# Where ScalarE writes an exp whose values nobody reads: SBUF rows in place of the PSUM bank it reads

## Chip, cores, metric

One core of a Trainium2 chip. The metric is device time in microseconds (us) of one execution; medians with lowest and highest are given.

## The reference

```python
def reference(x, bias):                       # x: (8, 2048, 2048) f32, bias: (8, 256)
    x_heads = x.reshape(B, S, H, Dh).transpose(0, 2, 1, 3)
    x_heads = x_heads + bias[None, :, None, :]
    x_tiled = np.repeat(x_heads, 2, axis=2)
    mx = x_tiled.max(axis=-1, keepdims=True)
    return mx.squeeze(-1) + np.log(np.exp(x_tiled - mx).sum(axis=-1))
```

A log of a sum of exps over each 256 elements of x + bias, every result given twice. The kernels take the exp without subtracting the maximum.

## The kernel before

It streams x, 134.2 MB, through nine SBUF buffers of 2 MiB: 64 blocks of 128 partitions x 2 rows x 2048 columns (8 heads of 256). The work on a block is split over the engines. In the first 49 blocks:

- Heads 0 and 1 ("ScalarE's own"): TensorE adds the bias by a bf16 matmul of ones with three bias parts, then an fp32 matmul of x with the identity into the same PSUM bank; ScalarE takes the exp, and the sum comes out of its accumulator.
- Heads 2 and 3: one large exp on ScalarE in place, VectorE multiplies by exp(bias) and sums.
- Heads 4 to 7: GpSimd adds the bias, the same large exp, VectorE sums.

Blocks 49 to 60 give ScalarE one head of its own, the last three blocks two.

```python
NBUF = 9
...
xts = [sb.tile([P, K, D], F32, name=f"xt{i}") for i in range(NBUF)]
ps = [pp.tile([P, MM], F32, name=f"ps{i}") for i in range(5)]     # five banks, in turn
...
def load(t):
    after = last_uses[t - NBUF] if t >= NBUF else []
    ...                                            # the load of block t waits for these
def add_bias(m, t, k0, k1):
    ...                                            # bias matmul, then x matmul, into bank p
        last_uses[t].append(on_x(t, mm, [loads[t, k0, 0]]))
    return got

def sum_biased(m, p, dst):
    for h in range(m["pe"]):
        c = h * Dh
        nc.scalar.activation(
            out=p[:, c : c + Dh],                  # in place in PSUM; never read
            in_=p[:, c : c + Dh],
            func=ACT.Exp,
            accum_out=dst(h),
        )
```

The softmax here doesn't subtract the row's maximum and nothing guards it: scores larger than these inputs give would overflow.

Of the kernel before, what the change touches and what calls it, by code (L numbers as in the profile page):

```python
# [16 lines left out]
NBUF = 9  # L17
# [15 lines left out]
def kernel(  # L33
# [6 lines left out]
    nc = tc.nc  # L40
    P = nc.NUM_PARTITIONS
    B, S, D = x.shape
    H, Dh = bias.shape
# [27 lines left out]
    xts = [sb.tile([P, K, D], F32, name=f"xt{i}") for i in range(NBUF)]  # L71
# [5 lines left out]
    def mode_of(t):  # L77
        return [m for t0, m, _ in STAGES if t0 <= t][-1]
# [4 lines left out]
    def pieces(t):  # L83

        if not halves_of(t):
            return [(0, K, 0, D)]
        cuts = [[0, D]] * K if t < T - 1 else LAST_CUTS
        return [
            (k, k + 1, c0, c1) for k in range(K) for c0, c1 in zip(cuts[k], cuts[k][1:])
        ]  # L90
# [13 lines left out]
    def on_x(t, ins, after):  # L104
        known = [u for u in users[t] if u.ins.engine != ins.ins.engine]
        for before in range(t % NBUF, t, NBUF):
            known += users[before]
        for u in known:
            if u not in after:
                tc.declare_no_dep(  # L110
                    ins.ins, u.ins, reason="waited for by those it waits for"
                )
        users[t].append(ins)
        return ins

    loads = {}

    last_uses = [[] for _ in range(T)]

    def load(t):  # L120
        after = last_uses[t - NBUF] if t >= NBUF else []
        for k0, k1, c0, c1 in pieces(t):
            loads[t, k0, c0] = on_x(
                t,
                nc.sync.dma_start(
                    out=xts[t % NBUF][:, k0:k1, c0:c1],
                    in_=rows_of(t)[:, k0:k1, c0:c1],
                ),
                after,
            )  # L130
# [37 lines left out]
    for i, c in enumerate(range(G0, D, MM)):  # L168
        spread(ps[i], c, c + MM)
        nc.scalar.activation(  # L170
            out=b_rep[:, c - G0 : c - G0 + MM], in_=ps[i], func=ACT.Copy
# [9 lines left out]

    def add_bias(m, t, k0, k1):

        n = m["pe"] * Dh
        xt = xts[t % NBUF]
        step = MM // n
        groups = [(k, min(k + step, k1)) for k in range(k0, k1, step)]
        got = []
        for ka, kb in groups:
            p = ps[n_ps[0] % len(ps)]  # L190
            n_ps[0] += 1
            nc.tensor.matmul(  # L192
                p[:, 0 : (kb - ka) * n],
                lhsT=ones3,
                rhs=each_row(b3, 0, n, kb - ka),
                start=True,
                stop=False,
            )
            got += [p[:, k * n : (k + 1) * n] for k in range(kb - ka)]
        for ka, kb in groups:  # L200
            p = got[ka - k0]
            mm = nc.tensor.matmul(  # L202
                bass.AP(
                    tensor=p.tensor,
                    offset=p.offset,
                    ap=[p.ap[0], [1, (kb - ka) * n]],
                ),
                lhsT=ident,
                rhs=xt[:, ka:kb, 0:n],
                start=False,  # L210
                stop=True,
            )
            last_uses[t].append(on_x(t, mm, [loads[t, k0, 0]]))
        return got

    def sum_biased(m, p, dst):
        for h in range(m["pe"]):
            c = h * Dh
            nc.scalar.activation(  # L219
                out=p[:, c : c + Dh],  # L220
                in_=p[:, c : c + Dh],
                func=ACT.Exp,
                accum_out=dst(h),
            )

    def each_row(src, c, n, k_rows):

        return bass.AP(
            tensor=src.tensor,
            offset=src.offset + c,  # L230
            ap=[src.ap[0], [0, k_rows], [1, n]],
        )

    def g_add(m, t, k0, k1):
        c = m["g0"] * Dh
        v = xts[t % NBUF][:, k0:k1, c:D]
        add = nc.gpsimd.tensor_tensor(  # L237
            out=v, in0=v, in1=each_row(b_rep, c - G0, D - c, k1 - k0), op=ALU.add
        )
        return on_x(t, add, [loads[t, k0, 0]])  # L240

    def exp_inplace(t, v, after):
        return on_x(t, nc.scalar.activation(out=v, in_=v, func=ACT.Exp), [after])  # L243

    def later(m, t, k0, k1, sums, add):

        h0 = m["pe"] if m["late"] else m["g0"]
        v = xts[t % NBUF][:, k0:k1, h0 * Dh : D]
        done = exp_inplace(t, v, add)
        if m["late"]:  # L250
            n = (m["g0"] - h0) * Dh
            f = v[:, :, 0:n]
            mul = nc.vector.tensor_tensor(  # L253
                out=f,
                in0=f,
                in1=each_row(w_ps, h0 * Dh - W0, n, k1 - k0),
                op=ALU.mult,
            )
            done = on_x(t, mul, [done])
        red = nc.vector.tensor_reduce(  # L260
            out=sums[:, k0:k1, h0:H],
            in_=v.rearrange("p k (h j) -> p k h j", j=Dh),
            op=ALU.add,
            axis=mybir.AxisListType.X,
        )
        last_uses[t].append(on_x(t, red, [done]))

    def weigh(t, v, h, dst, after):
        c = h * Dh
        w = w_ps[:, c - W0 : c - W0 + Dh] if c < W1 else w_sb[:, c - W1 : c - W1 + Dh]  # L270
        ttr = nc.vector.tensor_tensor_reduce(  # L271
            out=v,
            in0=v,
            in1=w,
            scale=1.0,
            scalar=0.0,
            op0=ALU.mult,
            op1=ALU.add,
            accum_out=dst,
        )  # L280
        last_uses[t].append(on_x(t, ttr, [after]))

    def finish(b):

        nr = H * NBLK
        tp = tps[b % 2]
        for k in range(K):
            nc.tensor.transpose(  # L288
                out=tp[0:nr, k],
                in_=R[b][:, k].rearrange("p h n -> p (h n)"),  # L290
                identity=ident,
            )
        tv = bass.AP(
            tensor=tp.tensor,
            offset=tp.offset,
            ap=[[tp.ap[0][0], nr], [1, P], [P, K], [0, 2]],
        )
        nc.scalar.activation(out=res[:, b], in_=tv, func=ACT.Ln)  # L298
# [23 lines left out]
    def sums_of(t):  # L322

        b, blk = divmod(t, NBLK)
        if b < B - 1:
            return R[b][:, :, :, blk]
        return R_last[:, :, blk, :].rearrange("p h k -> p k h")
# [3 lines left out]
    for t in range(T):  # L331
        m = mode_of(t)
        xt = xts[t % NBUF]
        sums = sums_of(t)
        for k0, k1, c0, c1 in pieces(t):
            add = None
            if c0 == 0:
                got = add_bias(m, t, k0, k1)
                if m["g0"] < H:
                    add = g_add(m, t, k0, k1)  # L340
            if for_pool:
                for_pool()
                for_pool = None
            h0 = max(c0 // Dh, m["pe"])
            h1 = min(c1 // Dh, m["g0"])
            if h0 < h1 and not m["late"]:
                done = exp_inplace(
                    t, xt[:, k0:k1, h0 * Dh : h1 * Dh], loads[t, k0, c0]
                )
            if for_pe and (c0 == 0 or c1 == D):  # L350
                for_pe()
                for_pe = None
            if not m["late"]:
                for k in range(k0, k1):
                    for h in range(h0, h1):
                        weigh(
                            t,
                            xt[:, k, h * Dh : (h + 1) * Dh],
                            h,
                            sums[:, k, h : h + 1],  # L360
                            done,
                        )

            def pool_part(t=t, m=m, k0=k0, k1=k1, sums=sums, add=add):
                if add:
                    later(m, t, k0, k1, sums, add)
                if k1 == K and t + NBUF < T:
                    load(t + NBUF)

            def pe_part(m=m, got=got, k0=k0, k1=k1, sums=sums):  # L370
                for k in range(k0, k1):
                    sum_biased(m, got[k - k0], lambda h: sums[:, k, h : h + 1])

            for_pool = pool_part
            if c0 == 0:
                if m["g0"] < H:
                    pe_part()
                else:
                    for_pe = pe_part

        fb, at = divmod(t - 2, NBLK)
        if fb >= 0 and at == NBLK - 1:
            finish(fb)
            if fb == B - 2:
                store()
# [34 lines left out]
```

## Time and profile before

| | kernel before |
|---|---|
| time, median (lowest to highest) | 329.37 us (329.17 to 329.44), 6 runs |
| span of the profiled run | 327.8 us |
| queue of the loads | 97.7% of the 16 DMA engines' time |
| ScalarE (ACT) busy | 290.7 us (89%) |
| VectorE (DVE), GpSimd (POOL), TensorE (PE) busy | 288.2, 270.7, 224.6 us |

Busy times of engines lie beside each other; none of them is the time. The lines behind the table stand in the prediction, with how they are read.

### The profile page before, as it was taken

How to read it: one execution, taken by the hardware profiler on the slowest of the kernel's cores; microseconds unless marked ns; L12 is line 12 of the kernel's file. 1: busy time of each engine (PE TensorE's matmuls, PEld its weight loads, DVE VectorE, ACT ScalarE, POOL GpSimd, SP SyncE). 2: the span in 40 equal slices, each digit the busy share in tenths (PEclk: the TensorE clock that was granted, in tenths of full speed). 3: DMA queues.
4: the chain of work that ended last, by engine and by line, in shares of the span. 5: the costliest groups of instructions: out<-in, count | busy, mean ns of one | idle time of the engine just before them, and what ended most of it. 6: DMA issues, size and time to landing. Idle time of an engine off the chain costs nothing.

```text
span 327.8 us, 1984 instructions
## 1 busy us (share of the span) xinstructions
PE 224.6 (68%) x383; PEld 65.2 (20%) x383; DVE 288.2 (88%) x380; ACT 290.7 (89%) x567; POOL 270.7 (83%) x79
## 2 busy tenths in 40 slices
PE   5497856667687668947897767687657546576793
PEld 2032211122122212211221211122212101122220
DVE  0009999999999999989999999999998999999994
ACT  3269999999999998999989899999998998999894
POOL 6999989979999999999998999999989668687300
PEclk9999798598967895698558777967897555555555
DMA  7999999999999999999999999999999999999991
GB/s 291 438 426 436 419 430 432 426 432 420 432 430 425 436 420 431 426 430 433 420 434 421 431 430 420 436 426 428 434 419 436 426 428 419 421 420 425 415 386 40
DMA packets 11646, 135.41 MB, mean 413 GB/s; under 512 B 1329, under 2 KB 1457, under 8 KB 2673
## 3 DMA queue, kind: packets, MB, share of 16 engines
q1 hardware_dynamic: 11536, 135.27, 97.7%
q8 instruction: 3, 0.05, 0.1%
q14 instruction: 9, 0.07, 0.1%
q10 hardware_dynamic: 2, 0.01, 0.0%
q0 software_dynamic: 96, 0.00, 0.0%
HBM read 134.23 MB, written 1.05 MB: 413 GB/s over the span
## 4 chain that ended last, share of the span: by engine, by line
DMA 66%; DVE 21%; ACT 4%; PE 4%; POOL 3%; issue 0%; SPq 0%; DVEq 0%
DMA xt<-in_x_dram 64%; DVE R L260 15%; DVE xt L253 5%; PE ps L202 3%; ACT xt L243 3%; DMA b<-bparts 2%; POOL xt L237 1%; ACT ps L219 1%; DMA brow<-in_bias_dram 1%; DVE xt L271 1%; PE ps L192 1%; POOL brest L157 0%; POOL brest L155 0%; POOL b L160 0%; POOL bparts L156 0%
## 5 line engine op out<-in xcount | busy, mean ns | idle before, releaser
L237 POOL TENSOR_TENSOR xt<-xt,b_rep 128x2048 f32<-128x2048 f32 (+2 forms) x65 | 264.3, 4069 | 33.2 <-DMA xt<-in_x_dram 33.2
L202 PE MATMUL ps<-xt,ident 128*128 128x512 f32 (+1 forms) x240 | 172.1, 848 | 77.4 <-DMA xt<-in_x_dram 77.1
L243 ACT ACTIVATE xt<-xt 128x3072 f32<-128x3072 f32 (+3 forms) x89 | 184.7, 2095 | 9.1 <-POOL xt L237 7.2
L260 DVE TENSOR_REDUCE R<-xt 128x12 f32<-128x3072 f32 (+1 forms) x56 | 176.6, 3154 | 1.7
L219 ACT ACTIVATE ps<-ps 128x256 f32<-128x256 f32 x232 | 85.7, 369 | 15.4 <-PE ps L202 11.4
L253 DVE TENSOR_TENSOR xt<-xt,w_ps 128x1024 f32<-128x1024 f32 x49 | 59.6, 1217 | 32.6 <-ACT xt L243 32.5
L202 PEld LDWEIGHTS ps<-xt,ident 128*128 128x128 f32 x240 | 53.3, 251 | 157.0 <-DMA xt<-in_x_dram 116.0
L192 PE MATMUL ps<-b,ones 3*128 3x512 bf16 (+1 forms) x120 | 47.1, 456 | 10.6 <-ACT ps L219 6.6
L219 ACT ACTIVATION_READ_ACCUMULATOR ps<-ps 128x1 f32 x232 | 44.1, 190 | 0.0
L271 DVE CUSTOM_DVE_ANT_0 xt<-xt,w_ps 128x256 f32<-128x256 f32 x114 | 40.4, 413 | 0.7 <-ACT xt L243 0.7
L192 PEld LDWEIGHTS <-ones 3*128 3x128 bf16 x120 | 7.8, 97 | 78.6 <-issue 78.6
L260 DVE TENSOR_REDUCE R_last<-xt 128x3 f32<-128x768 f32 (+1 forms) x9 | 9.3, 1036 | 0.0
L288 PE MATMUL tpair<-ident,R 128*64 128x128 f32 x14 | 3.7, 361 | 6.2 <-DVE R L260 6.2
L271 DVE CUSTOM_DVE_ANT_0 xt<-xt,w_sb 128x256 f32<-128x256 f32 x18 | 6.6, 416 | 0.0
L164 PE MATMUL ps<-brow,ones 1*128 1x512 f32 x4 | 3.7, 1085 | 3.4 <-DMA brow<-in_bias_dram 3.4
L271 DVE DVE_READ_ACCUMULATOR2_ANT R_last<- 128x1 f32 x76 | 6.0, 79 | 0.0
L170 ACT ACTIVATE b_rep<-ps 128x512 f32<-128x512 f32 x2 | 1.2, 598 | 4.5 <-PE ps L164 4.5
L271 DVE DVE_READ_ACCUMULATOR2_ANT R<- 128x1 f32 x56 | 4.6, 82 | 0.0
L164 PE MATMUL w_ps<-brow,ones 1*128 1x512 f32 x4 | 4.0, 1094 | 0.7 <-ACT w_ps L176 0.7
L288 PEld LDWEIGHTS tpair<-ident,R 128*64 128x64 f32 x14 | 1.6, 140 | 12.6 <-DVE R L260 10.0
L176 ACT ACTIVATE w_ps<-w_ps 128x512 f32<-128x512 f32 x2 | 1.2, 582 | 3.3 <-PE w_ps L164 3.3
L298 ACT ACTIVATE res<-tpair 64x512 f32<-64x512 f32 x7 | 4.0, 577 | 0.0
(21 smaller groups left out, 12.4 us busy)
## 6 DMA issues: line engine op xcount, KB each, us to landing
xt<-in_x_dram SPq DMA_DIRECT2D x57, 2048.0 KB, 31.9
xt<-in_x_dram SPq DMA_DIRECT2D x12, 1024.0 KB, 24.7
out_dram<-res SPq DMA_DIRECT2D x1, 896.0 KB, 9.8
xt<-in_x_dram SPq DMA_DIRECT2D x3, 256.0 KB, 14.4
xt<-in_x_dram SPq DMA_DIRECT2D x2, 384.0 KB, 16.1
xt<-in_x_dram SPq DMA_DIRECT2D x1, 512.0 KB, 12.2
out_dram<-res_last SPq DMA_DIRECT2D x1, 128.0 KB, 1.7
b<-bparts POOLq DMA_DIRECT2D x3, 1.0 KB, 5.9
```

The source lines that it names most:

```text
L164: nc.tensor.matmul(dst, lhsT=ones, rhs=brow[:, c0:c1], start=True, stop=True)
L170: nc.scalar.activation(out=b_rep[:, c - G0 : c - G0 + MM], in_=ps[i], func=ACT.Copy)
L192: nc.tensor.matmul(p[:, 0 : (kb - ka) * n], lhsT=ones3, rhs=each_row(b3, 0, n, kb - ka), start=True, stop=False,)
L202: mm = nc.tensor.matmul(bass.AP(tensor=p.tensor, offset=p.offset, ap=[p.ap[0], [1, (kb - ka) * n]],), lhsT=ident, rhs=xt[:, ka:kb, 0:n], s ...
L219: nc.scalar.activation(out=p[:, c : c + Dh], in_=p[:, c : c + Dh], func=ACT.Exp, accum_out=dst(h),)
L237: add = nc.gpsimd.tensor_tensor(out=v, in0=v, in1=each_row(b_rep, c - G0, D - c, k1 - k0), op=ALU.add)
L243: return on_x(t, nc.scalar.activation(out=v, in_=v, func=ACT.Exp), [after])
L253: mul = nc.vector.tensor_tensor(out=f, in0=f, in1=each_row(w_ps, h0 * Dh - W0, n, k1 - k0), op=ALU.mult,)
L260: red = nc.vector.tensor_reduce(out=sums[:, k0:k1, h0:H], in_=v.rearrange("p k (h j) -> p k h j", j=Dh), op=ALU.add, axis=mybir.AxisListTy ...
L271: ttr = nc.vector.tensor_tensor_reduce(out=v, in0=v, in1=w, scale=1.0, scalar=0.0, op0=ALU.mult, op1=ALU.add, accum_out=dst,)
L288: nc.tensor.transpose(out=tp[0:nr, k], in_=R[b][:, k].rearrange("p h n -> p (h n)"), identity=ident,)
L298: nc.scalar.activation(out=res[:, b], in_=tv, func=ACT.Ln)
```

## The change

The exp of ScalarE's own heads is an output that nobody reads; only its sum is wanted. The change sends it to the columns of x it came from, in SBUF, rather than back into the PSUM bank. The intent is to make the bank something that ScalarE only reads. In exchange ScalarE becomes a user of the x buffer, so the next load into it waits for ScalarE in place of the matmul. The core of the diff:

```diff
@@ add_bias @@
-            got += [p[:, k * n : (k + 1) * n] for k in range(kb - ka)]
+            got.append([p[:, k * n : (k + 1) * n] for k in range(kb - ka)])
 ...
-            last_uses[t].append(on_x(t, mm, [loads[t, k0, 0]]))
-        return got
-
-    def sum_biased(m, p, dst):
+            on_x(t, mm, [loads[t, k0, 0]])
+            rows += [(v, mm) for v in views]
+        return rows
+
+    def sum_biased(m, t, k, p, mm, sums):
+
         for h in range(m["pe"]):
             c = h * Dh
-            nc.scalar.activation(
-                out=p[:, c : c + Dh],
+            act = nc.scalar.activation(
+                out=xts[t % NBUF][:, k, c : c + Dh],
                 in_=p[:, c : c + Dh],
                 func=ACT.Exp,
-                accum_out=dst(h),
-            )
+                accum_out=sums[:, k, h : h + 1],
+            )
+            last_uses[t].append(on_x(t, act, [mm]))
```

More of the change, by code (lines that the diff above doesn't have):

```diff
@@ L198, in add_bias @@
             )
-            got += [p[:, k * n : (k + 1) * n] for k in range(kb - ka)]
-        for ka, kb in groups:
-            p = got[ka - k0]
+            got.append([p[:, k * n : (k + 1) * n] for k in range(kb - ka)])
+        rows = []
+        for (ka, kb), views in zip(groups, got):
+            p = views[0]
             mm = nc.tensor.matmul(
@@ L368, in pool_part, with pe_part @@
                     load(t + NBUF)
-            def pe_part(m=m, got=got, k0=k0, k1=k1, sums=sums):
+            def pe_part(t=t, m=m, got=got, k0=k0, k1=k1, sums=sums):
                 for k in range(k0, k1):
-                    sum_biased(m, got[k - k0], lambda h: sums[:, k, h : h + 1])
+                    sum_biased(m, t, k, *got[k - k0], sums)
             for_pool = pool_part
```

## The prediction

> **What bounds the kernel now.** I read the page from the top: busy shares, traffic by slice, queue shares.
>
> ```profile
> PE 224.6 (68%) x383; PEld 65.2 (20%) x383; DVE 288.2 (88%) x380; ACT 290.7 (89%) x567; POOL 270.7 (83%) x79
> GB/s 291 438 426 436 419 430 432 426 432 420 432 430 425 436 420 431 426 430 433 420 434 421 431 430 420 436 426 428 434 419 436 426 428 419 421 420 425 415 386 40
> q1 hardware_dynamic: 11536, 135.27, 97.7%
> ```
>
> ScalarE has the largest busy share of the compute engines, which makes the change look like one to the bottleneck. The two lines below it say otherwise: from the second slice of 8.2 us to the last but one the traffic stays between 386 and 438 GB/s, and the queue of the loads takes 97.7% of the time of the 16 DMA engines. No engine reaches that. Next the busy time by stage, to see whether the rate of the transfers depends on what the engines do (columns: stretch, then us in it, busy us and instructions of PE, PEld, DVE, ACT, POOL, granted clock, DMA share, GB/s).
>
> ```profile
> 8.00:16.00 8.00, 3.34 (x5) 0.63 (x4) 0.00 (x0) 1.91 (x3) 7.98 (x5) 1.00 1.00 426
> 16.00:25.00 9.00, 9.00 (x18) 2.76 (x16) 1.04 (x1) 5.59 (x14) 8.40 (x3) 1.00 1.01 433
> 25.00:87.00 62.00, 41.58 (x83) 12.14 (x82) 61.51 (x28) 60.99 (x124) 56.60 (x13) 0.86 1.01 428
> 87.00:165.00 78.00, 57.10 (x98) 16.67 (x98) 73.97 (x34) 73.17 (x150) 72.34 (x17) 0.75 1.01 428
> 165.00:295.00 130.00, 85.67 (x145) 24.52 (x144) 123.07 (x183) 119.73 (x219) 111.15 (x29) 0.70 1.01 426
> ```
>
> With ScalarE 24% busy (1.91 of 8.00 us) the rate is 426 GB/s; with ScalarE 98% busy (60.99 of 62.00) it is 428. Neither the load on ScalarE nor its SBUF traffic shows in it. 134.2 MB at 428 GB/s is 314 us, which is nearly the 315.2 us at which the last load on the chain lands. So the time is loads, and about 12.6 us of tail behind them.
>
> Then whether loads can ever be late, from the waits of the DMA queue's own issuer and the table of issues (KB each, us to landing):
>
> ```profile
> SPq L125 <- DVE R L260: 233.6, 50, 19.2
> xt<-in_x_dram SPq DMA_DIRECT2D x57, 2048.0 KB, 31.9
> ```
>
> A load is issued when the reduction on VectorE frees its buffer (233.6 us of waiting), but then takes 31.9 us to land, and at 428 GB/s a block of 2 MiB takes 4.90 us. So 31.9 / 4.90 = 6.5 blocks are in flight of nine buffers. A release would have to come some 27 us late before the DMA engines ran dry.
>
> **What the change touches.** Line 219 on ScalarE, 232 heads. In the steady part (time order: start, us, what):
>
> ```profile
> 154.07 0.37 ACT L219 ACTIVATE ps<-ps 128x256 f32<-128x256 f32 x1
> ...
> 154.58 0.37 ACT L219 ACTIVATE ps<-ps 128x256 f32<-128x256 f32 x1
> ...
> 154.96 0.38 ACT L219 ACTIVATE ps<-ps 128x256 f32<-128x256 f32 x1
> ...
> 155.47 0.37 ACT L219 ACTIVATE ps<-ps 128x256 f32<-128x256 f32 x1
> ```
>
> The starts are 0.51, 0.38 and 0.51 us apart. The lists of instructions of the two built programs tell why they alternate: in the kernel before, the second head of each bank waits for ScalarE's own semaphore, because its in-place output lies in the bank that the first head wrote. In the changed kernel that wait is gone: 114 ScalarE instructions waited for their own engine before (112 of them second heads), none after. The orders on TensorE, VectorE and GpSimd are the same; on the issuing queue the order is the same, and the loads wait for ScalarE where they waited for TensorE.
>
> **What the Trainium skill says.** "ScalarE: Activation LUTs", section "Step-by-step: what each stage is for", says that ScalarE writes faster to PSUM than to SBUF; by it the change goes the wrong way. "Perfetto Trace Analysis", section "Optimizing Scalar/DVE Operations", puts the access overhead of ScalarE at about 93 ns on SBUF and 51 ns on PSUM, 42 ns apart. The trace agrees with the direction but shows less (busy us, mean ns):
>
> ```profile
> L219 ACT ACTIVATE ps<-ps 128x256 f32<-128x256 f32 x232 | 85.7, 369 | 15.4 <-PE ps L202 11.4
> L170 ACT ACTIVATE b_rep<-ps 128x512 f32<-128x512 f32 x2 | 1.2, 598 | 4.5 <-PE ps L164 4.5
> L176 ACT ACTIVATE w_ps<-w_ps 128x512 f32<-128x512 f32 x2 | 1.2, 582 | 3.3 <-PE w_ps L164 3.3
> L315 ACT ACTIVATE res_last<-tpair 128x256 f32<-128x256 f32 x1 | 0.4, 384 | 1.2 <-PE tpair L309 1.2
> ```
>
> For 512 elements out of PSUM, a write to SBUF takes 598 ns and one to PSUM 582; for 256 elements 384 and 369. The destination alone costs 15 to 16 ns. "SBUF — State Buffer", section "Who interferes with whom", says that DMA has ports of its own and never contends with a compute engine; the stages above agree (426 to 433 GB/s). "DMA: Bandwidth & Descriptors", section "Where 436 GB/s comes from", gives a ceiling of 435 GB/s for the ports into SBUF; the trace's 428 is 98% of it, so nothing is left to win there.
>
> **The change part by part.**
> - Removed: 112 waits of ScalarE for itself, 0.51 - 0.38 = 0.13 us each: 14.6 us of ScalarE's time.
> - Added: 232 writes to SBUF in place of PSUM at 15 ns: 3.5 us, if all of it lies between starts. As the read of the accumulator already starts 0.28 to 0.30 us after its ACTIVATE and so overlaps the 0.37, I expect most of it not to.
> - Busy time: about 0.03 us of each 0.13 was an uncounted gap (the read of 0.18 to 0.19 us after 154.37 ends before 154.58), so 112 x 0.10 = 11 us of busy time go and up to 3.5 come back. ACT should show about 280 us in place of 290.7.
> - Moved: what frees a buffer. A block's heads end about 156 us in the stretch above, its large exp starts at 156.31 and its reduction ends at 163.7, so ScalarE's new claim is over some 7 us before the old one that counts. No load is issued later for it.
> - On the path: between the first block and 315 us, nothing. In the stage from 25 to 87 us, where the kernel catches up on its late start, the chain runs through VectorE without a gap (61.51 of 62.00 us busy), and VectorE's work is not changed; afterwards each block waits for its load.
>
> The tail is where ScalarE stands on the chain: from 315.25 us, where a large exp starts on landed data, to 321.88, where the last row of VectorE work starts.
>
> ```profile
> 317.81 2.08 PE L202 MATMUL ps<-xt,ident 128*128 128x512 f32 x2
> 318.43 1.56 ACT L243 ACTIVATE xt<-xt 128x768 f32<-128x768 f32 x2
> ...
> 319.92 0.37 ACT L219 ACTIVATE ps<-ps 128x256 f32<-128x256 f32 x1
> ...
> 320.81 1.56 ACT L243 ACTIVATE xt<-xt 128x1024 f32<-128x1024 f32 x2
> ...
> 321.88 0.42 DVE L271 CUSTOM_DVE_ANT_0 xt<-xt,w_ps 128x256 f32<-128x256 f32 x1 [0.44 <-ACT xt L243]
> ```
>
> Ahead of 321.88 lie three pairs of heads (starting at 316.64, 317.54 and 319.92), so three waits of 0.13 us, 0.39 us at most. But TensorE, at clock 0.50, ends the matmuls for the third pair at 317.81 + 2.08 = 319.89. ScalarE starts that pair at 319.92 today and would be ready for it 0.26 us earlier; it will wait there for TensorE instead. Only the third pair's own wait is left: 0.13 us. The last pair (322.46) is off the chain already. VectorE has 0.44 us to spare before 321.88, so it passes the 0.13 on.
>
> Sum: 329.38 - 0.13 = 329.25 us; I say **329.2**.
>
> **Rivals.**
> 1. ScalarE is the bound and its 11 us come off the time: about 318 us. For it: 89%, the largest share. Against it: the loads' 97.7%, and 314 us of transfers that no ScalarE time shortens. I give it under 1%.
> 2. The write to SBUF costs the skill's 42 ns between starts and nothing is won from the waits. ScalarE's work for a block is then 2.66 us (large exp, 61.60 to 64.26 us elsewhere in the trace) plus 2 x (0.51 + 0.38) + 4 x 0.042 = 4.61 us, under the 4.90 us of a block's load: hidden still, though above VectorE's 4.51 us a block (25.22 to 29.73) while catching up. In the tail six heads would add 0.25 us: 329.6.
> 3. ScalarE's 30 MB of new writes (232 x 128 KiB) into the rows that DMA fills slow the loads. One per cent of rate would be 3.1 us: 332.5. The stages speak against it, since the large exps write far more to SBUF (L243: 184.7 us of work) at an unchanged 428.
> 4. The third pair in the tail isn't held by TensorE (a higher clock at that stage): the full 0.39 us comes off, 329.0.
>
> **Range and chances.** Rivals 2 and 4 span 329.0 to 329.6. The three runs of before span 0.27 us, and executions otherwise differ by about 0.3%, which is 1 us and outweighs every step above. So 328.3 to 330.2. A 2% change is 6.6 us, which no step can make: faster 0.01, slower 0.01.
>
> **What would show it.** Right: load queue still near 97.7%, stages at 426 to 433 GB/s, starts of heads 0.38 us apart throughout, the heads' ACTIVATE at about 384 ns, ACT busy near 280 us with its idle time grown by as much and ended by GpSimd, TensorE or loads; and in the tail a pair of heads waiting for TensorE. Wrong: a lower GB/s in stages where heads run, heads still 0.51 us apart, loads whose issuer waits for ScalarE, or a span outside 325 to 331 us.

## The result and the profile after

329.25 us (328.67 to 329.45, 6 runs) after 329.37 (329.17 to 329.44, 6 runs). The ratio is 0.9994, 95% interval 0.9981 to 1.0007: the same. Here and below a ratio is the mean time of one kernel's runs over that of the other's of the same rounds, so it isn't quite the ratio of the medians quoted.

First the page of the changed kernel: busy times, traffic by slice, queue of the loads.

```profile
PE 227.0 (69%) x383; PEld 66.3 (20%) x383; DVE 288.4 (88%) x380; ACT 278.1 (85%) x567; POOL 270.8 (83%) x79
GB/s 293 431 428 434 427 426 428 428 424 432 426 426 431 426 430 425 426 432 425 424 433 424 423 432 426 430 430 424 428 429 422 434 428 416 422 418 423 420 394 52
q1 hardware_dynamic: 11536, 135.27, 97.8%
```

ScalarE lost 12.6 us of busy time (290.7 to 278.1). TensorE shows 2.4 us more (224.6 to 227.0), VectorE and GpSimd are within 0.2 us, and the load queue stays where it was (97.7%, now 97.8%). By stage (columns as in the prediction):

```profile
25.00:87.00 62.00, 42.34 (x80) 12.45 (x79) 61.55 (x28) 58.05 (x127) 56.99 (x13) 0.84 1.01 428
87.00:165.00 78.00, 57.62 (x100) 16.74 (x100) 73.43 (x33) 68.90 (x146) 72.27 (x17) 0.76 1.01 428
165.00:295.00 130.00, 87.69 (x143) 25.09 (x142) 122.86 (x182) 114.34 (x217) 111.02 (x29) 0.67 1.01 426
```

ScalarE is 3, 4 and 5 us less busy in the three stages; the rates, 428, 428 and 426 GB/s, are those of before. Then four heads of one block in order of time (start, us, what), to be held against the four in the prediction:

```profile
158.75 0.36 ACT L223 ACTIVATE xt<-ps 128x256 f32<-128x256 f32 x1
...
159.11 0.37 ACT L223 ACTIVATE xt<-ps 128x256 f32<-128x256 f32 x1
...
159.46 0.38 ACT L223 ACTIVATE xt<-ps 128x256 f32<-128x256 f32 x1
...
159.82 0.39 ACT L223 ACTIVATE xt<-ps 128x256 f32<-128x256 f32 x1
```

The steps are 0.36, 0.35 and 0.36 us where they were 0.51, 0.38 and 0.51. Counted over the whole trace, where no other engine was waited for between a head and the next, 113 of 150 steps were 0.50 to 0.53 us before, among them all 112 within a bank; now 139 of 144 are 0.35 to 0.38. The mean step within a bank fell from 0.516 to 0.361 us.

Last the tail, third pair of heads and what follows:

```profile
317.64 1.94 PE L204 MATMUL ps<-xt,ident 128*128 128x512 f32 x2
317.94 1.57 ACT L248 ACTIVATE xt<-xt 128x768 f32<-128x768 f32 x2
...
319.62 0.38 ACT L223 ACTIVATE xt<-ps 128x256 f32<-128x256 f32 x1
...
320.35 1.57 ACT L248 ACTIVATE xt<-xt 128x1024 f32<-128x1024 f32 x2
...
321.44 0.42 DVE L276 CUSTOM_DVE_ANT_0 xt<-xt,w_ps 128x256 f32<-128x256 f32 x1 [0.34 <-ACT xt L248]
```

ScalarE is done with the two exps of 768 at 317.94 + 1.57 = 319.51 and then stands until 319.62, because TensorE ends at 317.64 + 1.94 = 319.58: the pair now waits for TensorE, as foretold. From the start of this pair to VectorE's last row it takes 321.44 - 319.62 = 1.82 us; before it was 321.88 - 319.92 = 1.96. So this tail gives 0.14 us. The rest of the 0.44 us by which VectorE's last row came sooner isn't the change's: the pair itself started 0.30 us sooner, because TensorE began its two matmuls 0.17 us sooner (317.64 and 317.81) and took 1.94 instead of 2.08 us for them; the clock granted from 315 us on was 0.63 in the mean after and 0.50 before.

The chain that ended last shows whose tail this is in the changed kernel (start, us, what):

```profile
287.61 19.82 DMA xt<-in_x_dram
307.43 0.04 issue
307.48 2.08 PE ps L204 x2
...
317.71 1.89 PE ps L204 x2
319.59 0.02 issue
319.62 0.84 ACT xt L223 x4
```

From 307.48 to 319.59 us it runs through TensorE. In the kernel before, the profile draws it through ScalarE from 315.25 us on, but by a hair: TensorE is recorded without a pause from 315 to 322 us there as well, and the third pair started 0.03 us after TensorE's end (319.92 and 319.89), the same distance as here. So the tail was nearly TensorE's already, and this is why two of the three waits in it were worth nothing.

### The profile page after: what moved, and what is told of

It reads as the page before. It is cut to its first block, busy times and chain, and to the rows that moved or that the text cites. A ratio compares the mean times of both kernels' runs of the same rounds, so it can differ in the third digit from the quotient of the medians.

```text
span 327.4 us, 1988 instructions
## 1 busy us (share of the span) xinstructions
PE 227.0 (69%) x383; PEld 66.3 (20%) x383; DVE 288.4 (88%) x380; ACT 278.1 (85%) x567; POOL 270.8 (83%) x79
## 3 DMA queue, kind: packets, MB, share of 16 engines
q1 hardware_dynamic: 11536, 135.27, 97.8%
## 4 chain that ended last, share of the span: by engine, by line
DMA 57%; DVE 24%; PE 6%; POOL 6%; ACT 5%; issue 1%; SPq 0%; DVEq 0%
DMA xt<-in_x_dram 54%; DVE R L265 17%; DVE xt L258 6%; PE ps L204 5%; ACT xt L248 4%; POOL xt L242 4%; DMA b<-bparts 2%; PE ps L193 1%; ACT xt L223 1%; DMA brow<-in_bias_dram 1%; DVE xt L276 1%; POOL brest L157 0%; POOL brest L155 0%; POOL b L160 0%; POOL bparts L156 0%
## 5 line engine op out<-in xcount | busy, mean ns | idle before, releaser
L204 PE MATMUL ps<-xt,ident 128*128 128x512 f32 (+1 forms) x240 | 175.2, 863 | 80.9 <-DMA xt<-in_x_dram 80.6
L223 ACT ACTIVATE xt<-ps 128x256 f32<-128x256 f32 x232 | 86.7, 398 | 15.6 <-PE ps L204 15.1
L204 PEld LDWEIGHTS ps<-xt,ident 128*128 128x128 f32 x240 | 54.4, 256 | 157.3 <-DMA xt<-in_x_dram 117.5
L223 ACT ACTIVATION_READ_ACCUMULATOR xt<-ps 128x1 f32 x232 | 51.3, 223 | 0.0
```

The lines of the kernel that those rows point to most:

```text
L204: mm = nc.tensor.matmul(bass.AP(tensor=p.tensor, offset=p.offset, ap=[p.ap[0], [1, (kb - ka) * n]],), lhsT=ident, rhs=xt[:, ka:kb, 0:n], s ...
L223: act = nc.scalar.activation(out=xts[t % NBUF][:, k, c : c + Dh], in_=p[:, c : c + Dh], func=ACT.Exp, accum_out=sums[:, k, h : h + 1],)
```

## Experiments

Eight kernels ran, each beside the kernel before on the same chip.

### 1. The wait put back, SBUF kept

Both heads of a bank write the same columns, so the second must wait for the first again.

```diff
-                out=xts[t % NBUF][:, k, c : c + Dh],
+                out=xts[t % NBUF][:, k0_of(t, m, k), 0:Dh],
```

> The changed kernel with both heads of a bank writing the same columns of x, so that the second waits for the first again. Theory (the wait was all that the change removed from ScalarE): starts of heads 0.51 and 0.38 us apart in turn as in the kernel before, ACT busy about 291 us (278 in the changed kernel), 112 waits back. Rival (the gain on ScalarE comes from the destination): starts stay near 0.36 us and ACT busy stays near 278. Both expect the time of the kernel before within 0.3% (328.4 to 330.4 us), as ScalarE isn't the bound.

329.45 us (329.36 to 329.75), before 329.42; ratio 1.0006 (0.9989 to 1.0022). ACT busy is 288.8 us. One block in order of time:

```profile
153.93 0.37 ACT L226 ACTIVATE xt<-ps 128x256 f32<-128x256 f32 x1
...
154.41 0.38 ACT L226 ACTIVATE xt<-ps 128x256 f32<-128x256 f32 x1
...
154.79 0.38 ACT L226 ACTIVATE xt<-ps 128x256 f32<-128x256 f32 x1
...
155.29 0.38 ACT L226 ACTIVATE xt<-ps 128x256 f32<-128x256 f32 x1
```

Steps of 0.48, 0.38 and 0.50 us: the pattern of before is back with the output still in SBUF. The wait accounts for 288.8 - 278.1 = 10.7 of the 12.6 us; the remaining 1.9 us (290.7 - 288.8) go with the destination. Over the whole trace the step within a bank is 0.497 us in the mean (0.516 before, 0.361 in the changed kernel). In the tail it takes 1.96 us again from the start of the third pair to VectorE's last row (319.68 to 321.64).

### 2. Half of the heads back in PSUM, without the wait for the head just before

```diff
-    ps = [pp.tile([P, MM], F32, name=f"ps{i}") for i in range(5)]
+    ps = [pp.tile([P, MM], F32, name=f"ps{i}") for i in range(4)]
+    junk = pp.tile([P, MM], F32, name="junk")
-                out=xts[t % NBUF][:, k, c : c + Dh],
+                out=junk[:, 0:Dh] if odd_of(m, k, h) else xts[t % NBUF][:, k, c : c + Dh],
```

> The changed kernel with the second head of each bank written to a spare PSUM bank (four banks for matmuls in place of five), so no head waits for the one just before it. Theory (the destination costs 15 ns of recorded length and nothing between starts): the step from a head to the next start is 0.35 to 0.38 us behind SBUF heads and behind PSUM heads alike, with a difference under 10 ns; recorded lengths about 369 ns for PSUM and 377 or more for SBUF. Rival (a write to SBUF costs the engine 42 ns more than one to PSUM): steps behind SBUF heads 0.04 us longer. Time within 0.4% of before for both; one bank less could make ScalarE wait for TensorE a little more.

329.83 us (329.58 to 329.87), before 329.42; ratio 1.0013 (0.9998 to 1.0028). ACT busy 280.1 us, and as expected it waited a little more for TensorE with one bank less (17.8 us; 15.1 in the changed kernel). Part of one block:

```profile
158.90 0.36 ACT L227 ACTIVATE xt<-ps 128x256 f32<-128x256 f32 x1
159.16 0.19 ACT L227 ACTIVATION_READ_ACCUMULATOR xt<-ps 128x1 f32 x1
159.25 0.37 ACT L227 ACTIVATE junk<-ps 128x256 f32<-128x256 f32 x1
159.55 0.18 ACT L227 ACTIVATION_READ_ACCUMULATOR junk<-ps 128x1 f32 x1
```

Behind a head that writes SBUF its accumulator is read 0.26 us after its start, behind one that writes PSUM 0.30 us. Over the trace the step to the next start is 0.36 us in the median behind SBUF heads (112 steps) and 0.39 behind PSUM heads (63). Neither theory had that: the difference exceeds the 10 ns that mine allowed, and it is of the opposite sign to the rival's. It isn't the place in the bank: behind the same second heads, written to SBUF in the changed kernel, the step is 0.36 us. By starts, writing to SBUF out of PSUM is the shorter by some 0.03 us. By ends, which experiment 4 shows (for a large exp) to be what other engines see, it is some 0.02 us: 0.365 us from end to end behind SBUF heads, 0.386 behind PSUM heads. The PSUM heads aren't free of waits: 115 of the 116 wait for ScalarE's own semaphore. What they wait for is the head that wrote the spare bank last, not the head just before. The step up to them is 0.36 us all the same, as in the changed kernel, where no head waits for ScalarE; so this wait costs nothing that shows here. My 369 ns for PSUM heads was a miss as well: they are recorded at 383 in the mean, SBUF heads at 379.

### 3. and 4. More work on ScalarE, in both kernels

If the freed time is real, added work must fit into it.

```diff
+    junk = sb.tile([P, 768], F32, name="junk")
 ...
+        if not halves_of(t):
+            nc.scalar.activation(out=junk, in_=b_rep[:, 0:768], func=ACT.Exp)
```

> The kernel before with one more exp of 768 elements on ScalarE in each of the first 57 blocks, 0.74 us each, 42 us in all, whose result is not used. Theory (ScalarE is not the bound but has only 0.4 us to spare in a block of 4.90): 4.46 + 0.74 = 5.20 us a block, ScalarE becomes the bound, 345 to 356 us. Rival (ScalarE has much slack everywhere): within 1% of before.

351.15 us (351.00 to 351.23), before 329.42; ratio 1.0661 (1.0645 to 1.0677).

> The changed kernel with the same 42 us of extra exps. Theory (the change truly freed some 0.36 us of ScalarE in a block, which was only not needed): 2.66 + 4 x 0.355 + 0.74 = 4.82 us a block, just under the 4.90 of a load: 329 to 334 us, at least 12 us less than the same addition to the kernel before. Rival (the freed time is a matter of how the trace draws the instructions): as slow as extra_before within 1%.

333.99 us (333.00 to 334.11); ratio 1.0134 (1.0119 to 1.0149). The same stage, first of the kernel before with the extra exps, then of the changed one:

```profile
87.00:165.00 78.00, 52.66 (x94) 15.32 (x94) 68.48 (x30) 77.06 (x152) 72.23 (x17) 0.75 1.01 428
```

```profile
87.00:165.00 78.00, 56.37 (x101) 16.32 (x100) 73.00 (x33) 78.00 (x163) 71.78 (x17) 0.76 1.01 428
```

ScalarE is full in both (77.06 and 78.00 of 78), but the changed kernel does 163 instructions in the time of 152. VectorE's multiplications wait for the large exp, so their starts give the pace (first kernel, then changed one):

```profile
254.24 1.22 DVE L254 TENSOR_TENSOR xt<-xt,w_ps 128x1024 f32<-128x1024 f32 x1 [0.56 <-ACT xt L244]
259.41 1.22 DVE L254 TENSOR_TENSOR xt<-xt,w_ps 128x1024 f32<-128x1024 f32 x1 [0.56 <-ACT xt L244]
```

```profile
248.97 1.22 DVE L259 TENSOR_TENSOR xt<-xt,w_ps 128x1024 f32<-128x1024 f32 x1 [0.22 <-ACT xt L249]
253.80 1.22 DVE L259 TENSOR_TENSOR xt<-xt,w_ps 128x1024 f32<-128x1024 f32 x1 [0.22 <-ACT xt L249]
```

They are 5.17 us apart in the first and 4.83 in the second: 0.34 us a block freed for real, worth 17.2 us of time where ScalarE is the bound. The changed kernel with this work is still 4.6 us above before. The likely reason, which no run tested: every eighth step is longer, since ScalarE takes the logs of a batch there, and over all 48 steps the mean is 4.88 us, which hardly catches up with loads of 4.90 after ScalarE's late start.

A second thing is to be seen in the changed kernel with extra exps (instructions of one moment):

```profile
250.36 3.40 ACT L249 ACTIVATE xt<-xt 128x3072 f32<-128x3072 f32 x1
253.01 1.02 ACT L224 ACTIVATE xt<-ps 128x256 f32<-128x256 f32 x1
...
253.80 1.22 DVE L259 TENSOR_TENSOR xt<-xt,w_ps 128x1024 f32<-128x1024 f32 x1 [0.22 <-ACT xt L249]
```

A large exp is recorded at 3.40 us here and 2.76 elsewhere, a head at 1.02 and 0.36, and the head "starts" 0.75 us before the exp ahead of it ends. VectorE, which needs that exp, starts 0.04 us after its recorded end (250.36 + 3.40 = 253.76). So the ends are what others see, and the starts have run ahead of them. It builds up by 8 to 9 ns a head for as long as ScalarE doesn't stand still. In the changed kernel itself heads grow from 0.38 us at 22.85 us to 0.64 at 55.82, 31 heads later, and are back at 0.38 after the next gap. That lifts their mean there to 398 ns while the median is 377.

### 5. and 6. Fewer bytes, in both kernels

```diff
+    def cut(t, c0, c1):
+        return 1536 if t >= NBUF and (c0, c1) == (0, D) else c1
-                    out=xts[t % NBUF][:, k0:k1, c0:c1],
-                    in_=rows_of(t)[:, k0:k1, c0:c1],
+                    out=xts[t % NBUF][:, k0:k1, c0 : cut(t, c0, c1)],
+                    in_=rows_of(t)[:, k0:k1, c0 : cut(t, c0, c1)],
-        return on_x(t, nc.scalar.activation(out=v, in_=v, func=ACT.Exp), [after])
+        return on_x(t, nc.scalar.activation(out=v, in_=v, func=ACT.Exp, scale=0.0), [after])
```

> The kernel before, with three quarters of the columns loaded from the tenth block on (results wrong on purpose; the large exps take scale 0 so that stale columns stay finite). Theory (loads are the bound, with VectorE at 4.51 us and GpSimd at 4.54 us a block next behind them): loads end near 250 us and the time falls to about 316 us (311 to 321). Rival (ScalarE or another engine is the bound already): time unchanged within 1%.

317.29 us (316.55 to 317.75), results wrong; ratio to before 0.9628 (0.9610 to 0.9645).

> The changed kernel with the same lighter loads. Theory: VectorE and GpSimd are next, not ScalarE, so about 316 us again, within 1% of light_before. Rival (ScalarE is the bound right behind the loads): at least 8 us less than light_before.

316.23 us (316.12 to 316.49); ratio 0.9599 (0.9585 to 0.9613). One stage of each, the lightened kernel before first:

```profile
165.00:240.00 75.00, 55.57 (x97) 16.13 (x97) 74.24 (x34) 73.33 (x149) 75.00 (x18) 0.70 0.90 347
```

```profile
165.00:240.00 75.00, 50.17 (x97) 14.65 (x97) 74.36 (x34) 69.02 (x148) 75.00 (x18) 0.75 0.91 347
```

Fewer bytes make it 12 us faster, so the loads were the bound. The scale of 0 isn't what helped: large exps take 2754 ns with it and 2759 without. Then GpSimd (75.00 of 75) and VectorE (74.24) are full, and ScalarE with 73.33 is hardly less so; taking 4.3 us from it in this stage gives 1.1 us over the whole kernel, 0.3%. Even without the loads' bound the change has little to win, because two more engines stand right behind it.

### 7. and 8. Four buffers, in both kernels

The prediction leans on nine buffers hiding when a buffer comes free. With four they don't.

```diff
-NBUF = 9
+NBUF = 4
```

> The kernel before with four buffers for x in place of nine, so that the release of a buffer matters. Both expect it slower than before: the first four blocks land by about 20 us, the first buffer comes free at 28.6 us, so some 8 us without loads at the start, then about 12 us from landing to release and 7 us for a load in four buffers of 4.9 us each: 334 to 345 us.

364.84 us (364.61 to 365.99); ratio to before 1.1080 (1.1061 to 1.1099).

> The changed kernel with four buffers. Theory (ScalarE's new claim on a buffer ends some 7 us before VectorE's, so releases come no later, and at the start even sooner by 0.2 us a pair): the same as nbuf4_before or up to 2 us less, waits of the issuing queue still on the reduction of VectorE. Rival (the new claim of ScalarE on the buffer delays loads, which nine buffers had hidden): longer than nbuf4_before by over 1%, waits of the issuing queue on the heads' ACTIVATE.

365.19 us (363.72 to 367.05); ratio 1.1069 (1.1044 to 1.1093). The waits of the queue that issues the loads (total us, times, longest), kernel before with four buffers, then changed kernel:

```profile
SPq L125 <- DVE R L260: 295.6, 56, 25.2
```

```profile
SPq L125 <- DVE R L265: 295.8, 56, 24.7
SPq L125 <- ACT xt L248: 5.6, 17, 1.6
```

The size was a miss: I had put 7 us on a load from issue to landing, and it took 9.8 (10.0 in the changed kernel). What the pair was for holds in the main: both are equal within their intervals, and nearly all the waiting for a buffer is for VectorE in both. Not quite all: near the end, at 336.3 us, the issuer had VectorE's release and was then held 1.6 us by ScalarE, where the same load waits 0.3 us for TensorE in the kernel before with four buffers. The other waits for ScalarE are 0.4 us at most, as those for TensorE were. The runs of the changed kernel spread over 3.3 us, so a delay of that size can't be seen in the time.

## Why the prediction was right

- **The bound.** Loads at 97.7% and 426 to 433 GB/s, whatever ScalarE does: the same after (97.8%, 426 to 428), and shown by the lightened loads, the only edit here that made the kernel clearly faster.
- **The wait removed.** 14.6 us of starts was the estimate, of which 11 us busy; putting the wait back alone returned 10.7 us of busy time. Shown. By starts the 112 steps lost 17.4 us, (0.516 - 0.361) x 112; putting the wait back returned (0.497 - 0.361) x 112 = 15.2 of it, and the rest went with the destination.
- **The write to SBUF.** This term was wrong in sign. The prediction took 15 ns longer in the record for a cost and allowed up to 3.5 us; behind heads in SBUF the next head starts 0.03 us and ends 0.02 us sooner than behind heads in PSUM, and the destination alone was worth 1.9 us of busy time. The 15 ns were not read from the destination alone either: the lines compared differ in function too (a copy or a log beside an exp). Between the kernel before and experiment 1, which keep the same waits, the heads' mean length is 369 and 379 ns. In the changed kernel it came out at 377 ns in the median for the 384 foretold. As nothing of it is on the path, the time didn't feel it. ACT busy fell to 278.1 for the 280 foretold.
- **The tail.** 0.13 us, with the third pair held by TensorE: 0.14 in the trace, with that wait there. The prediction put ScalarE on the chain from 315.25 us; that was a near tie with TensorE, which holds the chain from 307.48 us after the change. Against runs that spread over 0.8 us the 0.13 can't be told in the time, so that the median fell 0.05 us from the forecast is luck.
- **The release of buffers.** The prediction named loads whose issuer waits for ScalarE as a sign against it. By the letter there are 29 such waits in the changed kernel, 6.8 us in all, none over 0.3 us; in the kernel before waits put down to TensorE stood at 5.2 us in 18, none over 0.4. Over all causes the issuer waited 284.4 us before and 285.6 after for these loads, so a label changed, not an amount; four buffers agree, but for the one load in the tail.
- **Rivals.** ScalarE as the bound is refuted twice: with some 12 us less busy time the time stays, and with fewer bytes and ScalarE's work unchanged it falls. The 42 us of added work did make ScalarE the bound; smaller amounts were not tried. A 42 ns cost to SBUF and slower loads were not seen. Why a head that writes PSUM holds the next one longer stays open; so does whether the drifting starts are the engine or the recorder.

## What to carry to other kernels

Before a change to the busiest engine, ask what its busy share is next to: here 89% stood beside a load queue at 97.7%, and freed time became idle time. An output that nobody needs should go where nothing depends on it: in place in a PSUM bank it made each second instruction wait for the first, and nothing in the waits by engine showed it, only the alternating steps of the starts did. To learn what freed time is worth, add the same work to both kernels and see which can take it.

## What the Trainium skill lacked or had wrong

- "ScalarE: Activation LUTs", section "Step-by-step: what each stage is for", calls PSUM the lower-latency destination. With the input in PSUM the runs show the reverse for pacing: the next instruction starts 0.36 us after a 256-element exp to SBUF and 0.39 after one to PSUM (0.365 and 0.386 from end to end). The recorded length of single instructions agrees with the page between the kernel before and experiment 1 (369 ns to PSUM, 379 to SBUF), but not within experiment 2 (383 and 379).
- "Perfetto Trace Analysis", section "Optimizing Scalar/DVE Operations", gives the overhead by memory space (about 93 and 51 ns for ScalarE) without saying whether source or destination counts. Changing the destination alone, with the same waits, moved the mean recorded length by 10 ns (369 to 379).
- I found on no page what it costs ScalarE to wait for its own previous instruction: a step of 0.48 to 0.53 us in place of 0.35 to 0.38 here.
- "Perfetto Trace Analysis", section "Per-instruction lifecycle: what the profiler-reported window actually captures", has the record run from the start in the engine's ALUs to the acknowledged write. It doesn't say that starts run ahead of ends on an engine that never stands still: by 8 to 9 ns a head here, until a head of 0.36 us is recorded at 1.02, which spoils mean durations.
